# Transposes three steps behind their scores in a pipelined attention trunk on one core

## The chip, the core and the metric

The kernel runs on one core of one Trainium2 chip. The metric is device time in microseconds (us). Over three runs the kernel before took 768.53 us in the median (767.16 to 770.72).

The engines in what follows: PE is TensorE's matmul (PEld its weight load), DVE is VectorE, ACT ScalarE, POOL GpSimd, and SP is SyncE, which here only issues DMAs.

## What is computed

One layer of a hybrid decoder trunk: sequence 1024, model width 1024, all in float32. One input projection feeds three kinds of heads of width 64, their outputs are gated and mapped back, the input is added, and the sum is normalised.

```python
u = rms_norm(x, attn_norm)
dq, dk, dv, sq, ckv, iq, ik, iw, rq, rk, rv, gate = split(u @ w_in)
# A: six differential heads, causal
a = softmax(q0 @ k0.T) - lam * softmax(q1 @ k1.T)      # per head
o_a = rms_norm(a @ v) * (1 - lam_init)
# B: six sparse heads: an indexer scores keys, each query keeps its top 256 of them
score = sum_h(relu(iq_h @ ik.T) * iw_h);  sel = top_k(score, 256)
o_b = softmax(q_lat @ c_sel.T) @ c_sel @ w_uv
# C: four retention heads in chunks of 128
y = silu(gate) * concat(o_a, o_b, o_c)
out = rms_norm(x + y @ w_out, final_norm)
```

## The kernel before

Each float32 product is split into a high and a low half, so that one block of a gemm costs three matmuls (L130 to L132 for the input projection, L1003 to L1005 for the output projection). The program hands its streams of work to a scheduler that fixes every engine's order before the run, from program order and a simulation of when operands are ready. `interleave` shares the streams out by costs that are written in the table `K`. Its entry `bufs` is `NST, NP, NPQ, NW, NHL, NHALF, NY`, the numbers of buffers in seven pools; `NP` is that of `pp` (second softmaxes of the differential heads, every softmax of the sparse heads, L91's `ptile`) and `NPQ` that of `pq` (first softmaxes of the differential heads, and some tiles of the retention).

In time the stages follow each other so (`run`): the norm and load of the input to 51 us; first gemms and the indexer's scores to 160; then the six differential heads, the top-k search on DVE and ACT, and the other gemms side by side to about 500; the sparse heads for the second half of the queries beside the ties of the top-k, the output weights' loads and the start of the retention to 587; the sparse heads for the first half beside the rest of the retention and the first blocks of the output projection to 711; and the rest of the projection to the end.

Both kinds of attention go through `attend`, a software pipeline over steps. A step is one head and one block of 128 queries; two such blocks make a group (`GB`). At step t the program emits, in this order:

- the scores of step t into a PSUM tile `pS` (L718 in `diff`, L787 and L788 in `dsa`; two such tiles exist),
- the transposes of the probabilities of step t-2 into PSUM tiles `pB` (L678; two exist), each copied to the SBUF tile `pt` by ACT or DVE (L113, L115; `pt` has two buffers),
- `comb` of step t-1: reciprocals and scaling. For `diff` that is DVE's L743, POOL's scaling of `pq` (L744), and DVE's L745, L746 and L747, which forms the difference in `pp`; for `dsa` L801 and L803,
- `soft` of step t: a DVE instruction adds the mask and takes the row's extremum (L729, or L795 in `dsa`), ACT takes the exponential (L731, or L796),
- where step t-2 ended a group, the value product (L693) of that group: up to 15 matmuls from `pt` into a `pB` tile. In `dsa` DVE multiplies the result with the gate (L825).

The value product's matmuls keep their written order; everything else on PE is placed by the scheduler, with gemm matmuls between. `wide` (L298) borrows attention buffers early for raw weights. `project` loads the gated outputs as `yr` (L988, on SP's queue, where `out_weights` issues its loads of `w_out` at L969 and the heads issue their stacks at L383), splits them on ACT and multiplies (L1003).

Of the kernel before, what the change touches and what calls it, by code (L numbers as in the profile page):

```python
# [28 lines left out]
    0, 384, 768, 1152, 1536, 1664, 2176, 2248, 2504, 2760, 3016)  # L29
WA = 384 + 72  # L30
C_R = (C_RQ, C_RK, C_RV)
K = {'mk': 'up ky', 'mp': 's2 g5 g4', 'rt': ('hl', 'pq'), 's0': ('gg', 'ag', 'gg', 'ag', 'gg', 'ag', 'gg', 'ag'), 'xp': 2, 'bufs': (8, 3, 3, 5, 3, 4, 1), 'pp': (7,), 'rot': 0, 'order': 'g0 g1 k1 q1 k2', 'order2': 'q2 g2 rq g6 s0 ck g7 s1 M g3 rv rk | ', 'wd': 36, 'wt': 13, 'wg': 119, 'gw': 56, 'rw': 26, 'rx': 132, 'pw': 40, 'ow': 84, 'nf': 2, 'ev': 200, 'late': 8, 'de': ('aa', 'aa', 'aa'), 'da': 'ax', 'gd': (7, 4, 2), 'hlp': 'sqkk', 'tkp': '', 'vt': 'v', 'rs': 'x', 'nv': 1, 'dn': 'v', 'ws': 'gg', 'oe': ('av', 'gg'), 'one': 0, 'idx': (42, 40), 'iqs': 'iq2 iq3 q0 k0'}
NST, NP, NPQ, NW, NHL, NHALF, NY = K["bufs"]


# [33 lines left out]
class Trunk:  # L69
# [228 lines left out]
    def wide(self):  # L298
        self.dvw = []
        for k0 in range(0, KC, 2):  # L300
            tag, bufs = ("pq", NPQ) if k0 < 2 * NPQ else ("hl", NHL)
            raw = self.sb.tile([128, 2, WA], F, name=self.name("wr"), tag=tag, bufs=bufs)
            for j in ((0, 1), (1, 2)) if k0 < 2 else ((0, 2),):
                self.nc.scalar.dma_start(raw[:, j[0]:j[1]], self.i["w_dv"][
                    (k0 + j[0]) * 128:(k0 + j[1]) * 128].rearrange("(k p) c -> p k c", p=128))
            self.dvw.append(raw)

    def wsplit(self, c0, w):
        hs, ls = [], []
        if w == WA:  # L310
# [4 lines left out]
            ls = [big[2 + k // 2][:, k % 2] for k in range(KC)]  # L315
            self.split_w = lambda k: self.split(hs[k], ls[k], self.dvw[k // 2][:, k % 2], *K["s0"][k])
            return hs, ls
        n = 1024 // w
        for k0 in range(0, KC, n):
            h, l = (self.wtile("w" + x, [n, w]) for x in "hl")  # L320
            for j in range(0, n, n // 2):
                raw = self.rtile([n // 2, w])
                self.nc.sync.dma_start(raw, self.i["w_in"][0, (k0 + j) * 128:(k0 + j + n // 2) * 128,
                                                           c0:c0 + w].rearrange("(k p) c -> p k c", p=128))
                self.split(h[:, j:j + n // 2], l[:, j:j + n // 2], raw, *K["ws"])
            hs += [h[:, j] for j in range(n)]
# [3 lines left out]
    def evict(self, evac, *args):  # L330
        with self.tc.high_priority(offset=K["ev"]):
            evac(*args)
# [21 lines left out]
    def to_dram(self, key, n=2):  # L354
# [3 lines left out]
        def evac(half, ps):  # L358
            sl = slice(half * 512, half * 512 + 512)
            t = self.sb.tile([128, 2, 512], FR, name=self.name("hl"), tag="hl", bufs=NHL)  # L360
            if key[:2] in K["hlp"]:
                nc = self.nc
# [59 lines left out]
    def topk(self):  # L422
        nc = self.nc
        gd = K["gd"]
        ga = tuple(b for b in range(7, 1, -1) if b not in gd)
# [226 lines left out]
    def attend(self, pair, stages, GB=2, groups=(3, 2, 1, 0)):  # L652
        nc = self.nc
        steps = [(a, g, i) for a in range(2) for g in groups
                 for i in range(g * GB, g * GB + GB)]
        head, scores, soft, comb = stages
        pts, val = {}, {}
        W = GB * 128
        N = len(steps)
        hd = {}  # L660
        for t in range(N + 2):
            if t < N:
                a, g, i = steps[t]
                if a not in hd:
                    hd[a] = head(a)
                val[t] = scores(hd[a], i)
            if t >= 2:
                a, g, i = steps[t - 2]
                pr = val.pop(t - 2)
                if (g, a) not in pts:  # L670
                    pts[g, a] = self.sb.tile([128, NB, W], F, name=self.name("pt"), tag="pt", bufs=2)
                pt = pts[g, a]
                qo = (i - g * GB) * 128
                for k0 in range(0, i + 1, 4):
                    nk = min(4, i + 1 - k0)
                    p = self.pB((128, 4, 128))
                    for k in range(nk):
                        nc.tensor.transpose(p[:, k], pr[:, (k0 + k) * 128:(k0 + k + 1) * 128], self.ident)  # L678
                    self.cp(self.evac_eng[k0 // 4], pt[:, k0:k0 + nk, qo:qo + 128], p[:, :nk])
            if 0 <= t - 1 < N:  # L680
                val[t - 1] = comb(val[t - 1])
            if t < N:
                val[t] = soft(steps[t][2], val[t])
            if t >= 2 and steps[t - 2][2] % GB == GB - 1:
                a, g, i = steps[t - 2]
                o = self.pB((128, 128))
                h = 2 * pair + a
                vals = [self.v[:, k, h * 64:(h + 1) * 64] for k in range(i + 1)]
                with self.tc.manual_schedule(engines={mybir.EngineType.PE}):
                    for k in (i, *range(i)):  # L690
                        for u in (1, 0):
                            if k < i or u:
                                self.last = nc.tensor.matmul(  # L693
                                    o[u * 64:(u + 1) * 64], vals[k], pts[g, a][:, k, u * 128:(u + 1) * 128],
                                    start=k == (i if u else 0), stop=k == i - 1, skip_group_check=True)
                yield 0.5, (a, g, o)
            yield (steps[min(t, N - 1)][2] + 1) / 4.5, None
# [354 lines left out]
```

## Time and profile before

| | |
|---|---|
| median of three runs | 768.53 us (767.16 to 770.72) |
| profiled execution | 772.95 us, its span 771.2 us |
| PE busy | 718.2 us (93%) |
| PEld busy | 591.1 us (77%) |
| DVE busy | 559.9 us (73%) |
| ACT busy | 458.6 us (59%) |
| POOL busy | 310.4 us (40%) |
| chain that ended last | PE 62%, DVE 13%, DMA 8%, issue 7%, ACT 4%, POOL 4% |

Times of single instructions come from the one profiled execution. A busy share over the span is a mean over stages that differ; the page's 40 slices show DVE at nine tenths only from the eighth to the twenty-fourth, and PE near nine tenths through most of the span. "Waits" name the idle time in front of an instruction and the instruction that ended it.

### The profile page before, as it was taken

The numbers are of one execution on the slowest core, as the hardware profiler recorded it, in microseconds if no ns is written. First come the engines' busy times: TensorE is split into PE (matmuls) and PEld (weight loads), VectorE is DVE, ScalarE is ACT, GpSimd is POOL, SyncE is SP. The second block draws the span as 40 slices with busy tenths as digits, with TensorE's granted clock in tenths as the row PEclk, the third lists the DMA queues.
The fourth block names the chain that finished last, engine by engine and source line by source line (L and its number), as shares of the span: only waits on it lengthen the run. The fifth ranks groups of instructions, "written<-read, shape, count | busy, mean of one in ns | idle before, by whom it ended". The sixth has DMA issues, their size and how long they took to land.

```text
span 771.2 us, 12824 instructions
## 1 busy us (share of the span) xinstructions
PE 718.2 (93%) x4266; PEld 591.1 (77%) x4266; DVE 559.9 (73%) x1315; ACT 458.6 (59%) x1002; POOL 310.4 (40%) x343
## 2 busy tenths in 40 slices
PE   6999999999989999978889889999978999999996
PEld 5986788887878988756767668989756887777884
DVE  3684577989999989999889986426657775654443
ACT  4762555489687877786845655533355665653332
POOL 6422122434424539447347787337633332120000
PEclk9999999999999999999899989999979999999998
DMA  9716455472484344451383685565579964413441
GB/s 337 255 28 178 137 159 142 111 191 79 118 202 109 99 132 113 114 144 31 91 239 108 172 229 167 145 203 165 177 212 272 251 203 113 132 34 106 137 166 55
DMA packets 93618, 116.73 MB, mean 151 GB/s; under 512 B 11120, under 2 KB 62704, under 8 KB 93424
## 3 DMA queue, kind: packets, MB, share of 16 engines
q1 hardware_dynamic: 91152, 111.94, 50.8%
q10 hardware_dynamic: 2400, 3.97, 1.4%
q8 instruction: 34, 0.56, 0.3%
q14 instruction: 32, 0.26, 0.1%
HBM read 79.17 MB, written 36.18 MB: 150 GB/s over the span
## 4 chain that ended last, share of the span: by engine, by line
PE 62%; DVE 13%; DMA 8%; issue 7%; ACT 4%; POOL 4%; SPq 2%; ACTq 0%; DVEq 0%; POOLq 0%
PE pG L130 6%; PE pG L131 6%; PE pG L132 6%; PE pB L693 5%; PE pB L678 4%; PE pG L1003 4%; PE pG L1004 4%; PE pG L1005 4%; PE pS L272 3%; PE pG L347 2%; DVE jv L443 2%; PE pG L349 2%; PE pG L348 2%; PE pS L409 2%; PE pS L408 2%
## 5 line engine op out<-in xcount | busy, mean ns | idle before, releaser
L130 PE MATMUL pG<-uh,wh 128*128 128x512 f32 x352 | 142.5, 405 | 4.5 <-DVE gt L894 2.1
L132 PE MATMUL pG<-uh,wl 128*128 128x512 f32 x352 | 141.2, 401 | 1.7 <-POOL wl L123 1.7
L131 PE MATMUL pG<-ul,wh 128*128 128x512 f32 x352 | 140.4, 399 | 1.3 <-DVE ul L255 1.3
L123 POOL TENSOR_TENSOR wl<-wr,wh 128x512 fp32r<-128x512 f32 x56 | 79.9, 1443 | 84.4 <-PE pG L131 73.8
L457 ACT ACTIVATE ja<-sc,tk_c 128x896 int8<-128x896 f32 (+2 forms) x93 | 83.3, 896 | 22.3 <-DVE tk_c L464 16.5
L113 ACT ACTIVATE pt<-pB 128x512 f32<-128x512 f32 (+2 forms) x120 | 58.9, 496 | 41.9 <-PE pB L678 41.7
L130 PEld LDWEIGHTS pG<-uh,wh 128*128 128x128 f32 x352 | 67.5, 192 | 19.3 <-DVE gt L894 2.4
L132 PEld LDWEIGHTS pG<-uh,wl 128*128 128x128 f32 x352 | 67.4, 192 | 16.7 <-POOL wl L123 2.5
L131 PEld LDWEIGHTS pG<-ul,wh 128*128 128x128 f32 x352 | 67.4, 191 | 15.5 <-DVE ul L255 3.3
L678 PE MATMUL pB<-ident,pp 128*128 128x128 f32 x432 | 73.4, 288 | 4.6 <-DVE gt L825 1.9
L693 PE MATMUL pB<-pt,v 128*64 128x128 f32 x864 | 68.0, 294 | 7.4 <-ACT pt L113 6.8
L693 PEld LDWEIGHTS pB<-pt,v 128*64 128x64 f32 x864 | 55.3, 143 | 18.9 <-ACT pt L113 9.5
L443 DVE TENSOR_SCALAR_CACHE_REDUCE jv<-sc,tk_c 128x640 bf16<-128x640 f32 (+4 forms) x81 | 69.1, 853 | 0.9
L119 POOL TENSOR_SCALAR wh<-wr 128x512 fp32r<-128x512 f32 x56 | 40.3, 723 | 69.9 <-DMA wr<-in_w_in_dram 50.8
L678 PEld LDWEIGHTS pB<-ident,pp 128*128 128x128 f32 x432 | 51.7, 145 | 20.4 <-issue 8.5
L744 POOL TENSOR_SCALAR pq<-pq,mx 128x896 f32<-128x896 f32 (+7 forms) x48 | 39.2, 816 | 58.5 <-DVE mx L743 46.1
L347 PE MATMUL pG<-wh,uh 128*128 128x256 f32 x192 | 55.4, 290 | 0.7 <-POOL wh L119 0.7
L411 ACT ACTIVATE pp<-pS 128x1024 f32<-128x1024 f32 (+5 forms) x48 | 36.5, 760 | 31.5 <-PE pS L409 31.5
L348 PE MATMUL pG<-wl,uh 128*128 128x256 f32 x192 | 55.0, 287 | 0.0
L349 PE MATMUL pG<-wh,ul 128*128 128x256 f32 x192 | 54.4, 284 | 0.0
L747 DVE SCALAR_TENSOR_TENSOR pp<-pp,mx,pq 128x896 f32<-128x896 f32 (+7 forms) x48 | 51.1, 1065 | 4.4 <-POOL pq L744 3.6
L416 DVE SCALAR_TENSOR_TENSOR sc<-pp,iw,sc 128x1024 f32<-128x1024 f32 (+5 forms) x42 | 43.5, 1048 | 14.6 <-ACT pp L411 14.2
(234 smaller groups left out, 1731.4 us busy)
## 6 DMA issues: line engine op xcount, KB each, us to landing
wr<-in_w_in_dram SPq DMA_DIRECT2D x56, 256.0 KB, 3.1
st<-qdq SPq DMA_DIRECT2D x24, 256.0 KB, 4.2
st<-qkk SPq DMA_DIRECT2D x18, 256.0 KB, 6.1
qiq<-hl SPq DMA_DIRECT2D x16, 256.0 KB, 3.5
st<-qiq SPq DMA_DIRECT2D x8, 512.0 KB, 3.4
wr<-in_w_out_dram SPq DMA_DIRECT2D x16, 256.0 KB, 3.3
xr<-in_x_dram SPq DMA_DIRECT2D x8, 512.0 KB, 3.6
yr<-yd SPq DMA_DIRECT2D x7, 512.0 KB, 4.1
```

The source lines that it names most:

```text
L113: self.nc.scalar.activation(out, in_, AF.Copy)
L123: (self.nc.vector if e2 == "v" else self.nc.gpsimd).tensor_tensor(lo, src, hi.bitcast(F), OP.subtract)
L130: mm(ps, wh, xh, start=start, stop=False)
L131: mm(ps, wh, xl, start=False, stop=False)
L132: mm(ps, wl, xh, start=False, stop=stop)
L347: mm(ps, uh, hs[k], start=k == 0, stop=False)
L348: mm(ps, uh, ls[k], start=False, stop=False)
L349: mm(ps, ul, hs[k], start=False, stop=k == KC - 1)
L443: nc.vector.tensor_scalar(jv[:, :nv[b]], hb if b == 7 and bit >= 16 else sc[b], t, 0.0, op0=op, op1=OP.add, accum_out=cnt[:, j:j + 1])
L457: nc.scalar.activation(ja[:, :nv[b]], sc[b], AF.Sign, bias=cut(b), scale=-1.0, accum_out=cnt[:, cols[b]:cols[b] + 1])
L678: nc.tensor.transpose(p[:, k], pr[:, (k0 + k) * 128:(k0 + k + 1) * 128], self.ident)
L693: self.last = nc.tensor.matmul(o[u * 64:(u + 1) * 64], vals[k], pts[g, a][:, k, u * 128:(u + 1) * 128], start=k == (i if u else 0), stop=k ...
```

## The change

In `attend` a constant `L = 3` sets the distance of the transposes behind the scores, where 2 was written. A finished group is remembered in `done`, handed to `ready` at the next step, and its value product is emitted there: one step after the group's last transposes, at the same place in the step. The loop runs two more steps to empty the pipeline. `bufs` gives `pp` four buffers where it had three, and `pq` two where it had three. `wide` takes the third pair of raw weights from the `pp` pool instead of from `pq`. In the changed file L678 is L681, L693 is L698, and lines from 700 on stand five lower.

```diff
@@ -29,7 +29,7 @@
     0, 384, 768, 1152, 1536, 1664, 2176, 2248, 2504, 2760, 3016)
 WA = 384 + 72
 C_R = (C_RQ, C_RK, C_RV)
-K = {..., 'bufs': (8, 3, 3, 5, 3, 4, 1), ...}
+K = {..., 'bufs': (8, 4, 2, 5, 3, 4, 1), ...}
 NST, NP, NPQ, NW, NHL, NHALF, NY = K["bufs"]
 
 
@@ -298,7 +298,7 @@
     def wide(self):
         self.dvw = []
         for k0 in range(0, KC, 2):
-            tag, bufs = ("pq", NPQ) if k0 < 2 * NPQ else ("hl", NHL)
+            tag, bufs = (("pq", NPQ), ("pq", NPQ), ("p", NP), ("hl", NHL))[k0 // 2]
             raw = self.sb.tile([128, 2, WA], F, name=self.name("wr"), tag=tag, bufs=bufs)
             for j in ((0, 1), (1, 2)) if k0 < 2 else ((0, 2),):
                 self.nc.scalar.dma_start(raw[:, j[0]:j[1]], self.i["w_dv"][
@@ -658,15 +658,18 @@
         W = GB * 128
         N = len(steps)
         hd = {}
-        for t in range(N + 2):
+        L = 3
+        done = None
+        for t in range(N + L + 1):
             if t < N:
                 a, g, i = steps[t]
                 if a not in hd:
                     hd[a] = head(a)
                 val[t] = scores(hd[a], i)
-            if t >= 2:
-                a, g, i = steps[t - 2]
-                pr = val.pop(t - 2)
+            ready, done = done, None
+            if L <= t < N + L:
+                a, g, i = steps[t - L]
+                pr = val.pop(t - L)
                 if (g, a) not in pts:
                     pts[g, a] = self.sb.tile([128, NB, W], F, name=self.name("pt"), tag="pt", bufs=2)
                 pt = pts[g, a]
@@ -677,12 +680,14 @@
                     for k in range(nk):
                         nc.tensor.transpose(p[:, k], pr[:, (k0 + k) * 128:(k0 + k + 1) * 128], self.ident)
                     self.cp(self.evac_eng[k0 // 4], pt[:, k0:k0 + nk, qo:qo + 128], p[:, :nk])
+                if i % GB == GB - 1:
+                    done = (a, g, i)
             if 0 <= t - 1 < N:
                 val[t - 1] = comb(val[t - 1])
             if t < N:
                 val[t] = soft(steps[t][2], val[t])
-            if t >= 2 and steps[t - 2][2] % GB == GB - 1:
-                a, g, i = steps[t - 2]
+            if ready:
+                a, g, i = ready
                 o = self.pB((128, 128))
                 h = 2 * pair + a
                 vals = [self.v[:, k, h * 64:(h + 1) * 64] for k in range(i + 1)]
```

**PE, first head of the third pair of differential heads, the group of its last two query blocks.** The group's value product `L693` (`L698`) stands among scores (`L718`, `L723`), transposes (`L678`, `L681`) and gemm matmuls (`L130` to `L132`). Before:

```order
L678 MATMUL pB_3346<-ident,pp_3215 128x128 x4
L678 MATMUL pB_3352<-ident,pp_3215 128x128 x4
L718 MATMUL pS_3463<-st_3128,st_3125 128x384
L132 MATMUL pG_3573<-uh,wl_3488 128x512
L130 MATMUL pG_3573<-uh,wh_3487 128x512
L131 MATMUL pG_3573<-ul,wh_3487 128x512
L132 MATMUL pG_3573<-uh,wl_3488 128x512
L718 MATMUL pS_3510<-st_3121,st_3118 128x512
L693 MATMUL pB_3370<-pt_3298,v_158 64x128 x15
L678 MATMUL pB_3466<-ident,pp_3319 128x128 x4
```

After:

```order
L723 MATMUL pS_3560<-st_3106,st_3103 128x128
L131 MATMUL pG_3544<-ul,wh_3426 128x512
L132 MATMUL pG_3544<-uh,wl_3427 128x512
L130 MATMUL pG_3544<-uh,wh_3426 128x512
L131 MATMUL pG_3544<-ul,wh_3426 128x512
L132 MATMUL pG_3544<-uh,wl_3427 128x512
L723 MATMUL pS_3562<-st_3113,st_3110 128x128
L698 MATMUL pB_3509<-pt_3354,v_158 64x128 x15
L681 MATMUL pB_3564<-ident,pp_3375 128x128 x4
```

Before, the transposes of the group's last step (`pB_3346`, `pB_3352`, both from `pp_3215`) stand six rows ahead of the fifteen value matmuls. After, the last transposes that fill `pt_3354` (into `pB_3453`) stand 58 rows ahead of them.

**PE, the first matmul of the output projection**, where the sparse heads' first half of steps ends. `S` tiles of `L787` (`L792`) are scores, `woh` and `wol` the split output weights. Before:

```order
L787 MATMUL pS_6516<-st_6442,st_6440 128x512
L788 MATMUL pS_6516<-st_6444,st_6440 128x512
L787 MATMUL pS_6516<-st_6442,st_6440 128x256
L788 MATMUL pS_6516<-st_6444,st_6440 128x256
L693 MATMUL pB_6271<-pt_6258,v_5586 64x128 x3
L678 MATMUL pB_6496<-ident,pp_6453 128x128 x4
L787 MATMUL pS_6580<-st_6575,st_6573 128x512
L1003 MATMUL pG_6224<-woh,yh_6221 128x512
L1004 MATMUL pG_6224<-wol,yh_6221 128x512
```

After:

```order
L792 MATMUL pS_6158<-st_6137,st_6138 128x512
L793 MATMUL pS_6158<-st_6137,st_6138 128x512
L681 MATMUL pB_6146<-ident,pp_6102 128x128 x4
L1008 MATMUL pG_6195<-woh,yh_6192 128x512
L1009 MATMUL pG_6195<-wol,yh_6192 128x512
L506 MATMUL pG_6271<-rt_5614,bd 128x256
L792 MATMUL pS_6199<-st_6137,st_6138 128x128
L793 MATMUL pS_6199<-st_6137,st_6138 128x128
```

Before, the first projection matmul (`pG_6224`) stands behind the first score of the sixth step of the stage for the first half of the queries. After, it (`pG_6195`) stands before the last two scores of the stage ahead of that, seven score tiles earlier.

**SP's queue around the load of `yr`** (`L988`, `L993`), which that matmul needs. Before:

```order
L969 DMA wr_6044<-in_w_out_dram 128x512
L383 DMA st_6575<-qkk_4189 128x1024
L383 DMA st_6577<-qkk_4189 64x1024
L830 DMA yd_67<-gt_6146 128x1x128
L969 DMA wr_6068<-in_w_out_dram 128x512
L830 DMA yd_67<-gt_6146 128x1x128
L980 DMA fn_6215<-in_final_norm_dram 128x1024
L988 DMA yr_6217<-yd_68 128x3x128
L969 DMA wr_6072<-in_w_out_dram 128x512
```

After:

```order
L974 DMA wr_5939<-in_w_out_dram 128x512
L974 DMA wr_5994<-in_w_out_dram 128x512
L828 DMA gt_6182<-gd_3969 64x2x128
L835 DMA yd_67<-gt_5967 128x1x128 x2
L985 DMA fn_6186<-in_final_norm_dram 128x1024
L993 DMA yr_6188<-yd_68 128x3x128
L998 DMA xr_6190<-in_x_dram 128x1024
L974 DMA wr_5998<-in_w_out_dram 128x512
```

The load of `yr` stands behind 13 of the 16 loads of `w_out` before and behind 11 of them after, and `L383`'s loads of the last stage's first stacks stand ahead of it before, behind it after.

## Rows read from the trace of the kernel before

**Rows 1.** The page, busy time of each engine over the span, with instructions.
```profile
PE 718.2 (93%) x4266; PEld 591.1 (77%) x4266; DVE 559.9 (73%) x1315; ACT 458.6 (59%) x1002; POOL 310.4 (40%) x343
```

**Rows 2.** Busy time by stretch: PE, PEld, DVE, ACT, POOL, granted clock, DMA share.
```profile
190.00:320.00 130.00, 125.67 (x792) 105.78 (x791) 122.67 (x334) 101.17 (x236) 64.46 (x79) 0.99 0.48 126
320.00:454.00 134.00, 114.73 (x615) 89.34 (x614) 125.96 (x300) 91.36 (x212) 82.66 (x78) 0.92 0.51 137
454.00:515.00 61.00, 60.11 (x435) 52.57 (x431) 27.38 (x69) 31.02 (x75) 29.29 (x32) 1.00 0.60 177
560.00:590.00 30.00, 23.60 (x129) 16.67 (x129) 17.93 (x61) 17.58 (x46) 8.26 (x8) 0.77 0.84 234
590.00:711.00 121.00, 118.44 (x907) 96.22 (x907) 77.65 (x173) 68.87 (x150) 30.90 (x42) 1.00 0.52 150
```

**Rows 3.** PE's waits, 190 to 454 us: total us, times, longest.
```profile
PE pB L693 <- ACT pt L113: 6.3, 2, 3.5
PE pS L718 <- DVE mx L729: 4.3, 7, 0.9
...
PE pS L718 <- DMA qsq<-hl: 2.5, 1, 2.5
```

**Rows 4.** DVE's waits, 190 to 454 us.
```profile
DVE pp L729 <- PE pS L718: 2.6, 1, 2.6
...
DVE pq L729 <- PE pS L718: 2.3, 3, 1.7
...
DVE pp L747 <- POOL pq L744: 0.6, 1, 0.6
```

**Rows 5.** DVE's timeline, 363 to 382 us: start, length, instruction, idle before.
```profile
374.16 0.29 DVE L729 CUSTOM_DVE_ANT_0 pq<-pS,cb 128x128 f32<-128x128 f32 x1 [1.74 <-PE pS L718]
...
379.91 0.69 DVE L729 CUSTOM_DVE_ANT_0 pp<-pS,cb 128x512 f32<-128x512 f32 x1 [0.93 <-PE pB L678]
```

**Rows 6.** PE's timeline, 364 to 370 us.
```profile
369.01 1.39 PE L693 MATMUL pB<-pt,v 128*64 128x128 f32 x10 [3.51 <-ACT pt L113]
```

**Rows 7.** The page's costliest groups: two of POOL's.
```profile
L123 POOL TENSOR_TENSOR wl<-wr,wh 128x512 fp32r<-128x512 f32 x56 | 79.9, 1443 | 84.4 <-PE pG L131 73.8
...
L744 POOL TENSOR_SCALAR pq<-pq,mx 128x896 f32<-128x896 f32 (+7 forms) x48 | 39.2, 816 | 58.5 <-DVE mx L743 46.1
```

**Rows 8.** DVE's waits, 515 to 711 us.
```profile
DVE pp L795 <- PE pB L678: 8.0, 14, 1.6
```

**Rows 9.** PE's waits, 454 to 590 us.
```profile
PE pS L787 <- DVE mx L795: 1.9, 5, 0.7
PE pG L1003 <- ACT yh L113: 1.7, 1, 1.7
...
PE pB L693 <- ACT pt L113: 0.5, 1, 0.5
```

**Rows 10.** PE's waits, 590 to 720 us.
```profile
PE pS L787 <- DVE mx L795: 1.1, 2, 0.8
PE pB L678 <- ACT pt L115: 0.7, 1, 0.7
PE pB L693 <- DVE pt L115: 0.6, 1, 0.6
```

**Rows 11.** SyncE's DMA issues, 571 to 583 us.
```profile
573.87 0.33 SPq L969 DMA_DIRECT2D wr<-in_w_out_dram  x1
...
582.28 0.46 SPq L988 DMA_DIRECT2D yr<-yd  x1
```

**Rows 12.** PE's timeline, 571 to 592 us.
```profile
571.79 0.41 PE L788 MATMUL pS<-st,st 128*128 128x512 f32 x1
...
589.32 0.50 PE L1003 MATMUL pG<-woh,yh 128*128 128x512 f32 x1 [1.68 <-ACT yh L113]
```

**Rows 13.** ACT's timeline, 586 to 590 us.
```profile
588.74 0.52 ACT L113 ACTIVATE yh<-yr 128x384 fp32r<-128x384 f32 x1 [2.23 <-DMA yr<-yd]
```

More of the change, by code (lines that the diff above doesn't have):

```diff
@@ L31 @@
 C_R = (C_RQ, C_RK, C_RV)
-K = {'mk': 'up ky', 'mp': 's2 g5 g4', 'rt': ('hl', 'pq'), 's0': ('gg', 'ag', 'gg', 'ag', 'gg', 'ag', 'gg', 'ag'), 'xp': 2, 'bufs': (8, 3, 3, 5, 3, 4, 1), 'pp': (7,), 'rot': 0, 'order': 'g0 g1 k1 q1 k2', 'order2': 'q2 g2 rq g6 s0 ck g7 s1 M g3 rv rk | ', 'wd': 36, 'wt': 13, 'wg': 119, 'gw': 56, 'rw': 26, 'rx': 132, 'pw': 40, 'ow': 84, 'nf': 2, 'ev': 200, 'late': 8, 'de': ('aa', 'aa', 'aa'), 'da': 'ax', 'gd': (7, 4, 2), 'hlp': 'sqkk', 'tkp': '', 'vt': 'v', 'rs': 'x', 'nv': 1, 'dn': 'v', 'ws': 'gg', 'oe': ('av', 'gg'), 'one': 0, 'idx': (42, 40), 'iqs': 'iq2 iq3 q0 k0'}
+K = {'mk': 'up ky', 'mp': 's2 g5 g4', 'rt': ('hl', 'pq'), 's0': ('gg', 'ag', 'gg', 'ag', 'gg', 'ag', 'gg', 'ag'), 'xp': 2, 'bufs': (8, 4, 2, 5, 3, 4, 1), 'pp': (7,), 'rot': 0, 'order': 'g0 g1 k1 q1 k2', 'order2': 'q2 g2 rq g6 s0 ck g7 s1 M g3 rv rk | ', 'wd': 36, 'wt': 13, 'wg': 119, 'gw': 56, 'rw': 26, 'rx': 132, 'pw': 40, 'ow': 84, 'nf': 2, 'ev': 200, 'late': 8, 'de': ('aa', 'aa', 'aa'), 'da': 'ax', 'gd': (7, 4, 2), 'hlp': 'sqkk', 'tkp': '', 'vt': 'v', 'rs': 'x', 'nv': 1, 'dn': 'v', 'ws': 'gg', 'oe': ('av', 'gg'), 'one': 0, 'idx': (42, 40), 'iqs': 'iq2 iq3 q0 k0'}
 NST, NP, NPQ, NW, NHL, NHALF, NY = K["bufs"]
```

## The prediction

> **What bounds the kernel now.** I read the busy times first, then the stretches, then the waits of each stretch's bound. Over the span PE is busy 93% [rows 1], which would make it the bound everywhere. By stretch it isn't [rows 2]. From 190 to 454 us DVE is busy 122.67 of 130 and 125.96 of 134 us, 248.6 of 264, so that it idles 15.4; PE idles 4.3 + 19.3 = 23.6 there. From 454 to 515 PE is full (60.11 of 61) and DVE under half. From 560 to 590 nothing is full: PE 23.60 of 30, DVE 17.93, at a granted clock of 0.77, under the upper of PE's two levels (2.4 GHz is 1.00); there a chain of dependent steps sets the pace. From 590 to 711 PE is full again (118.44 of 121). So a saved wait counts on DVE in the stage of the differential heads, on PE behind it, and on whichever engine the chain stands at between 560 and 590.
>
> On PE's number the Trainium skill (Perfetto Trace Analysis, Identifying the Most-Contended Engine) says that the matmul row's busy share is a poor measure of how close an engine is to its limit, and that the weight loads' share is better. In the stretch that is full by its matmuls weight loads are busy 96.22 of 121, 80%, so 80% is about what "full" reads as here; by the rule as it stands 23% of the span (771.2 - 591.1 = 180 us) would be open, by the row 771.2 - 591.1/0.80 = 32 us. Neither enters the sum.
>
> **The change part by part.** All of it is counted against the profiled execution of 772.95 us; the median of the runs is 768.53, so its sums are multiplied by 0.9943 at the end.
>
> *The value product one step later, 190 to 454 us.* PE waited 6.3 us, twice, for ACT's copy into `pt` [rows 3]; one of the two is a 3.51 us wait at 369.01 [rows 6]. With the product a step behind its transposes the copy has a step more: in the order the last transposes stand 58 rows ahead of the product where they stood six ahead. I expect both waits gone. But DVE is the bound, so only what DVE lost through them counts: 1.74 us at 374.16 (it waits for a score that PE issued late) and 0.93 at 379.91 (for a transpose that frees a `pp` buffer) [rows 5]. Value -2.7; ends 0 (DVE has other work queued and the idle only moves) and -6.3 (PE's whole wait).
>
> *What stays there.* PE's waits for score tiles, 4.3 us in seven [rows 3], come from two `pS` tiles, which the change leaves at two: 0. DVE's longest wait, 2.6, is for a score that PE had to hold 2.5 for a DMA [rows 3, 4]; the loads of the stacks aren't altered, but any of them could shift: 0, ends -2.6 and +2.6.
>
> *The transposes three steps behind, with four `pp`.* A `pp` tile lives from `soft` of step t to the transposes of the same step. In program order two live at a time with distance 2, three with distance 3. Three buffers for two, or four for three, leave one spare either way. So DVE's waits for a `pp` buffer don't get rarer by the count alone; a transposed step merely finds `comb` done for longer, and in 190 to 454 PE's rows show no wait of a transpose for `comb` at all. Value 0; its cost, that PE's work at the end of the third pair comes two steps later, falls in 454 to 515, where PE is full of gemm matmuls that can go first: 0, end +5 if they run out (about two steps' transposes and products at the mean PE idle of such a step, by the 6.3 of [rows 3] the size of thing that can stand open).
>
> *Two `pq` for three.* Only one `pq` is alive in program order when the next is taken, so two suffice if POOL scales in time: POOL's scaling takes 816 ns in the mean, behind weight splits of 1443 [rows 7]. DVE waited 0.6 once for it [rows 4]. In DVE's order the median number of rows between the reciprocal that starts POOL and the combine falls from 15 to 10, and combines at seven rows or fewer go from 6 of 48 to 12. Ten rows at DVE's mean of 559.9/1315 = 0.43 us [rows 1] are 4.3 us, more than 1443 + 816 ns = 2.26. So the cover holds in most: the 0.6 doubles with the tight ones, +0.6. Ends: 0, and twelve tight combines that each lose 2.26 less three rows of cover (1.3), 12 x 0.96 = +11.5.
>
> *`wide` with a `pp` buffer.* The order on PE is the same up to about 190 us, so the early gemms hide it: 0. Should the `pp` tile come free late, the first of the sparse indexer's work would be held by one raw load; by the 2.5 us that a load held PE [rows 3], +2.5.
>
> *Sparse heads, 515 to 590.* PE waits 1.9 us in five for DVE to release a score tile, and 0.5 for ACT's copy into `pt` [rows 9]. DVE is late there because its own first instruction waits for transposes, 8.0 us in 14 [rows 8]: the transposes sit on PE behind the scores. With distance 3 they are of older, finished steps, and the order has them four score tiles behind their scores in the median, three before. So I take both waits as gone, -2.4; ends 0 (one spare buffer as before) and -6.4 (all of PE's 30 - 23.60 idle [rows 2]).
>
> *Sparse heads, 590 to 711.* Three waits of the same kinds, 1.1 + 0.7 + 0.6 [rows 10]: -2.4; ends 0 and -2.6 (PE's whole idle there).
>
> *The first projection matmul, which the order brings forward.* Before, it stood behind the first score of the next stage's sixth step and still waited 1.7 us [rows 9, 12] for ACT's split of `yr`, and ACT for the DMA until 588.74 [rows 13]. Its load was issued at 582.28 [rows 11], so it took 6.5 us to land. After, the load stands behind 11 `w_out` loads instead of 13, which is behind the issue at 573.87 [rows 11] and the stores and the `fn` load that keep their place there, about 575.5. It lands at 575.5 + 6.5 = 582.0, and the matmul could start 0.6 later (589.32 - 588.74), at 582.5. The matmul now stands seven score tiles earlier on PE, about where the score at 571.79 ends [rows 12], 572.2. PE is in order: scores of the two last steps and all their softmaxes queue behind it. If nothing else moves, it stalls 582.5 - 572.2 = 10.3 us. Against this: PE itself gets there later, since it waits at earlier places for the same DMAs and softmaxes (DMA engines are busy 0.84 [rows 2]), and part of the stall takes the place of the 6.4 us that PE idles there anyway. Ends -1.7 (the load is in time) and +10.3; I take +1.7, the old wait again, as the nearest row of the same instruction.
>
> *The sum.* -2.7 + 0.6 - 2.4 - 2.4 + 1.7 = -5.2: 772.95 - 5.2 = 767.75, times 0.9943 = 763.4 us, told as 763.
>
> **The rivals.**
>
> *Nothing happens.* DVE paces the stage from 190 to 454 and PE only waits somewhere else; the counts of spare buffers are the same as before, and the waits of 0.5 to 1.9 us reappear one instruction further on. Then 768.5, give or take 2. For it: DVE's 15.4 us of idle in 264, of which the value product explains 2.7. Against it: those 2.7 and the 4.8 behind 515 stand on the engine that bounds. The Trainium skill (Perfetto Trace Analysis, Optimization Strategy) says that a gap which repeats on the engine that should be full can mean that too few buffers are there for the next tile. By that rule the gap to mend is the one that repeats, PE's seven waits for `pS` (4.3 us), which the change doesn't touch; of the added `pp` buffer DVE's rows show one wait of 0.93 in the stage. The rule speaks for this rival.
>
> *The change doesn't do what it says* belongs to it: for the differential heads the scheduler put the transposes a median of four score tiles behind their scores in both orders, so that the distance written there is not the one executed.
>
> *The slow chain fills up.* If the older transposes free the pipeline between 560 and 590, PE's 6.4 us go, and its clock rises from 0.77 to 1.00, 23.60 x 0.23 = 5.4 more. With -2.7 and -2.4: -16.9, 756.05 x 0.9943 = 752. For it: four engines under 80% there. Against it: DMA at 0.84, which the change doesn't relieve.
>
> *Slower: the early projection matmul blocks PE.* The place is the matmul on `woh`, `yh` before the last two scores of the first sparse stage; the price is the 10.3 us above with no wait of 515 to 590 saved: -2.7 + 0.6 - 2.4 + 10.3 = +5.8, 778.75 x 0.9943 = 774.3. It decides once the stall exceeds about 8 us. For it: the order moves the matmul by seven score tiles, but its load by two of `w_out`. Against it: the load's 6.5 us came in a stretch with DMAs at 0.84 and can shrink.
>
> *Slower: `pq` runs short.* The +11.5 above in place of +0.6: 778.65 x 0.9943 = 774.2. It decides if POOL is behind a split at most of the tight combines. Against it: 0.6 us in all before.
>
> **How the numbers follow.** Forecast 0.36, nothing 0.24, the chain fills 0.15, the projection blocks 0.16, `pq` short 0.09. About 0.5% is what a measurement of this kernel can tell from no change: 764.7 and 772.4. The forecast's own range is 758 to 768, 0.26 of its 0.36 below 764.7. Faster 0.26 + 0.15 = 0.41; same 0.10 + 0.24 = 0.34; slower 0.16 + 0.09 = 0.25. The range goes from 752, the filled chain, to 777, 3 us above the slower rivals for their loose prices.
>
> **What the profile after would show.** Right: no wait of the value product (L698) for ACT's copy over 1 us between 190 and 454, and DVE's idle there near 12.7 instead of 15.4; fewer than 14 waits of L800 for transposes; L1008 waiting under 4 us. Wrong: L1008 waiting 8 or more; L752 waiting for POOL several times; the dsa stages' lengths unchanged with their waits merely renamed; or a stack's load that lands later and holds PE in the differential stage, which I cost at nothing.

## The result, and the profile after

The changed kernel took 777.51 us in the median of four runs (776.02 to 782.97) against 769.41 (767.16 to 770.72) in the same comparison: a ratio of 1.0108, 95% interval 1.0068 to 1.0148. It is slower by about 1%, where 763 was forecast. Its profiled execution took 776.35 us, against 772.95 before. So the two traces show 3.4 us of a difference that is 8.1 in the medians; what they show is where some of it went, and the ratios of the experiments carry the rest.

The page, busy time of each engine over the span, answering to [rows 1]:

```profile
PE 718.0 (93%) x4266; PEld 591.8 (76%) x4266; DVE 561.8 (73%) x1315; ACT 455.0 (59%) x1002; POOL 308.6 (40%) x343
```

Busy time by stretch, columns as in [rows 2]: PE, PEld, DVE, ACT, POOL, granted clock, DMA share, GB/s.

```profile
190.00:320.00 130.00, 122.39 (x763) 102.08 (x762) 121.11 (x337) 100.07 (x238) 62.60 (x79) 0.96 0.46 125
320.00:454.00 134.00, 121.09 (x660) 94.71 (x660) 128.77 (x298) 91.75 (x212) 85.49 (x80) 0.95 0.53 143
454.00:515.00 61.00, 60.02 (x435) 52.48 (x430) 27.14 (x72) 31.20 (x76) 27.39 (x30) 1.00 0.52 148
560.00:590.00 30.00, 25.06 (x155) 18.91 (x154) 21.56 (x68) 16.40 (x45) 10.54 (x13) 0.88 0.92 260
590.00:711.00 121.00, 114.62 (x859) 92.76 (x859) 74.72 (x174) 66.00 (x148) 25.42 (x36) 0.99 0.48 139
```

PE's busy time times its granted clock is, roughly, the work done at full clock (good to about a microsecond a row: the clock is a mean over the stretch, idle time included). From 190 to 320 us it was 125.67 x 0.99 = 124.4 before and is 122.39 x 0.96 = 117.5; from 320 to 454 it was 105.6 and is 115.0. Together PE did 2.5 us more by 454. From 590 to 711 it was 118.4 and is 113.5. The stretch in between, of before and then of after:

```profile
515.00:560.00 45.00, 43.09 (x345) 37.40 (x344) 29.33 (x88) 17.87 (x48) 29.20 (x41) 1.00 0.60 183
```

```profile
515.00:560.00 45.00, 39.24 (x312) 34.93 (x310) 28.89 (x79) 17.05 (x45) 30.69 (x42) 0.93 0.67 208
```

Here 43.1 us of work became 36.5; in the next stretch 18.2 became 22.1 [rows 2]. From 515 to 711 PE lost 6.6 - 3.9 + 4.9 = 7.6 us, three times what it had gained. Two single waits stand in these stretches, and the granted clock is at or near the lower level behind each: 0.50 from 555.7 to 560 us, 0.58 from 610.9 to 615.

```profile
555.70 2.15 PE L681 MATMUL pB<-ident,pp 128*128 128x128 f32 x8 [4.90 <-DVE gt L830]
610.89 0.75 PE L596 MATMUL pG<-rt 64*128 64x128 f32 x8 [3.76 <-ACT rt L589]
```

PE's waits from 190 to 454 us (total, times, longest), answering to [rows 3]:

```profile
PE pS L723 <- DVE mx L734: 5.5, 5, 2.3
PE pS L723 <- DVE jv L443: 3.3, 2, 3.0
...
PE pB L698 <- ACT pt L113: 0.2, 1, 0.2
```

The value product's 6.3 us are 0.2. The waits for score tiles stayed. DVE's waits in the same stretch, answering to [rows 4]:

```profile
DVE tk_n L462 <- ACT ja L457: 5.0, 4, 2.7
DVE pq L734 <- PE pS L723: 2.5, 3, 1.3
...
DVE pp L734 <- PE pB L681: 0.3, 1, 0.3
```

DVE's idle went from 15.4 to 264 - 121.11 - 128.77 = 14.1. PE's waits from 515 to 590, and from 590 to 711, answering to [rows 9] and [rows 10]:

```profile
PE pB L681 <- DVE gt L830: 7.5, 3, 4.9
...
PE pB L698 <- ACT pt L113: 0.8, 2, 0.5
...
PE pG L1008 <- ACT yh L113: 0.5, 1, 0.5
```

```profile
PE pG L596 <- ACT rt L589: 3.8, 1, 3.8
PE pS L792 <- DVE mx L800: 1.1, 1, 1.1
```

The wait of 7.5 us was 1.9 before. It is a transpose that wants a `pB` tile which still holds a value product; DVE multiplies that with a gate, and waited 4.1 us in all for gates to be loaded. The load is issued with the product, so a step later than before, but that isn't shown to be the reason: with the sparse heads' old loop the same wait is 3.9 us in e1, 4.4 in k2 and 6.0 in j1 (runs below). The 3.8 us are for a tile of the retention. DVE's waits for transposes in the sparse stages, 8.0 us in 14 before [rows 8], became 12.7 in 13; from 590 to 711 they are:

```profile
DVE pp L800 <- PE pB L681: 10.6, 10, 2.8
```

DVE's timeline at the end of the differential heads (the last combine, then the first sparse softmax):

```profile
498.88 0.48 DVE L752 SCALAR_TENSOR_TENSOR pp<-pp,mx,pq 128x256 f32<-128x256 f32 x1
511.33 0.56 DVE L800 CUSTOM_DVE_ANT_0 pp<-pS,sc 128x384 f32<-128x384 f32 x1 [11.97 <-PE pS L793]
```

The first sparse softmax waited 12 us for its score. Against the kernel before that is no loss. There DVE idled 16.3 us between the same two instructions, and the first sparse softmax came 4.3 us later:

```profile
497.44 0.48 DVE L747 SCALAR_TENSOR_TENSOR pp<-pp,mx,pq 128x256 f32<-128x256 f32 x1
509.38 0.69 DVE L507 TENSOR_SCALAR f<-pB 128x512 f32<-128x512 f32 x1 [11.45 <-PE pB L506]
511.44 0.75 DVE L513 SCALAR_TENSOR_TENSOR f<-f,c_diff_norm,f 128x512 f32<-128x512 f32 x1 [1.36 <-ACT f L509]
515.67 0.56 DVE L795 CUSTOM_DVE_ANT_0 pp<-pS,sc 128x384 f32<-128x384 f32 x1 [3.48 <-PE pS L788]
```

In PE's order 191 matmuls of the retention's gemms are left behind the first sparse score, where 288 were left before. But that count hangs on one matmul: before, the first of a score's two matmuls was issued alone, 15 us ahead of the second, and behind the second 191 are left too.

```profile
500.38 0.34 PE L787 MATMUL pS<-st,st 128*128 128x384 f32 x1
515.29 0.34 PE L788 MATMUL pS<-st,st 128*128 128x384 f32 x1
```

### The profile page after: what moved, and what is told of

It reads as the page before. It is cut to its first block, busy times and chain, and to the rows that moved or that the text cites. A ratio compares the mean times of both kernels' runs of the same rounds, so it can differ in the third digit from the quotient of the medians.

```text
span 774.6 us, 12837 instructions
## 1 busy us (share of the span) xinstructions
PE 718.0 (93%) x4266; PEld 591.8 (76%) x4266; DVE 561.8 (73%) x1315; ACT 455.0 (59%) x1002; POOL 308.6 (40%) x343
## 4 chain that ended last, share of the span: by engine, by line
PE 53%; DVE 23%; DMA 10%; issue 6%; ACT 3%; POOL 2%; SPq 1%; DVEq 0%; ACTq 0%; POOLq 0%
DVE jv L443 5%; PE pG L130 4%; PE pG L132 4%; PE pG L131 4%; PE pB L698 4%; PE pG L1008 4%; PE pG L1009 4%; PE pG L1010 4%; DVE pp L752 3%; PE pB L681 3%; PE pS L272 3%; DMA st<-qkk 2%; PE pG L348 2%; PE pG L347 2%; DVE pp L734 2%
## 5 line engine op out<-in xcount | busy, mean ns | idle before, releaser
L130 PE MATMUL pG<-uh,wh 128*128 128x512 f32 x352 | 143.9, 409 | 5.5 <-DVE gt L899 3.7
L132 PE MATMUL pG<-uh,wl 128*128 128x512 f32 x352 | 141.1, 401 | 2.9 <-POOL wl L123 2.9
L130 PEld LDWEIGHTS pG<-uh,wh 128*128 128x128 f32 x352 | 68.1, 194 | 21.4 <-issue 4.0
L681 PE MATMUL pB<-ident,pp 128*128 128x128 f32 x432 | 72.5, 286 | 9.7 <-DVE gt L830 7.5
L132 PEld LDWEIGHTS pG<-uh,wl 128*128 128x128 f32 x352 | 67.8, 193 | 17.6 <-POOL wl L123 3.3
L681 PEld LDWEIGHTS pB<-ident,pp 128*128 128x128 f32 x432 | 53.5, 146 | 23.1 <-DVE gt L830 8.2
L698 PE MATMUL pB<-pt,v 128*64 128x128 f32 x864 | 64.9, 284 | 2.5 <-ACT pt L113 1.8
L698 PEld LDWEIGHTS pB<-pt,v 128*64 128x64 f32 x864 | 52.3, 138 | 14.4 <-issue 6.1
L347 PE MATMUL pG<-wh,uh 128*128 128x256 f32 x192 | 55.1, 288 | 0.8 <-DVE mx L748 0.6
L411 ACT ACTIVATE pp<-pS 128x1024 f32<-128x1024 f32 (+5 forms) x48 | 36.5, 761 | 31.4 <-PE pS L409 31.4
L723 PE MATMUL pS<-st,st 128*128 128x512 f32 (+3 forms) x144 | 45.1, 383 | 10.5 <-DVE mx L734 5.5
L349 PE MATMUL pG<-wh,ul 128*128 128x256 f32 x192 | 54.4, 284 | 0.0
```

The lines of the kernel that those rows point to most:

```text
L130: mm(ps, wh, xh, start=start, stop=False)
L132: mm(ps, wl, xh, start=False, stop=stop)
L347: mm(ps, uh, hs[k], start=k == 0, stop=False)
L349: mm(ps, ul, hs[k], start=False, stop=k == KC - 1)
L698: self.last = nc.tensor.matmul(o[u * 64:(u + 1) * 64], vals[k], pts[g, a][:, k, u * 128:(u + 1) * 128], start=k == (i if u else 0), stop=k ...
```

## The experiments

All kernels but the one before and k3 have the new buffers unless told otherwise. "First sparse" is the start of the first sparse softmax in the trace, "left" the number of retention gemm matmuls (L347 to L349) that stand on PE behind the first matmul of a sparse score, and "left, third" behind the third such matmul.

| kernel | weight | loops, buffers | ratio to before, 95% | first sparse, us | left | left, third |
|---|---|---|---|---|---|---|
| before | 36 | old, pp 3, pq 3 | 1 | 515.7 | 288 | 191 |
| changed | 36 | new in both | 1.0108 (1.0068 to 1.0148) | 511.3 | 191 | 191 |
| e1 | 36 | new in differential heads | 1.0053 (1.0025 to 1.0081) | 513.9 | 191 | 191 |
| e2 | 36 | new in sparse heads | 0.9916 (0.9887 to 0.9946) | 486.5 | 360 | 191 |
| e3 | 36 | old | 0.9906 (0.9876 to 0.9937) | 488.4 | 360 | 191 |
| e4 | 36 | distance 3, no delay | 1.0127 (1.0097 to 1.0158) | 518.8 | 240 | 191 |
| f1 | 36 | old, pp 3, pq 2 | 1.0128 (1.0093 to 1.0162) | 516.4 | 191 | 191 |
| f2 | 36 | distance 2, delay, differential | 1.0102 (1.0069 to 1.0134) | 518.3 | 191 | 191 |
| g1 | 36 | new in third pair | 0.9990 (0.9959 to 1.0020) | 481.3 | 384 | 365 |
| g2 | 36 | new in first two pairs | 1.0006 (0.9974 to 1.0038) | 515.9 | 191 | 191 |
| j1 | 32 | old | 1.0158 (1.0134 to 1.0181) | 531.7 | 24 | 0 |
| j2 | 32 | new in both | 1.0268 (1.0223 to 1.0314) | 535.9 | 0 | 0 |
| j3 | 40 | old | 0.9924 (0.9896 to 0.9953) | 474.5 | 384 | 384 |
| j4 | 40 | new in both | 0.9923 (0.9899 to 0.9946) | 481.3 | 384 | 384 |
| k1 | 36 | new in both, drains free | 1.0100 (1.0064 to 1.0136) | 517.1 | 191 | 191 |
| k2 | 34.5 | old | 1.0014 (0.9994 to 1.0035) | 505.1 | 191 | 191 |
| k3 | 40 | old, pp 3, pq 3 | 1.0040 (1.0024 to 1.0057) | 492.4 | 360 | 240 |
| k4 | 36 | as f2, drain free | 1.0013 (0.9986 to 1.0039) | 511.5 | 191 | 191 |
| m2 | 36 | new in both, retention later | 1.0224 (1.0193 to 1.0256) | 489.5 | 348 | 348 |
| n1 | 32 | new in both, retention later | 1.0167 (1.0139 to 1.0196) | 505.5 | 254 | 254 |

**Which part loses.** After the traces, theory A was that the sparse heads' loop loses; B, the buffers; C, any new order. The edit of e1 (e2 has the two pairs of numbers exchanged, e3 has (2, 0) for both, e4 has (3, 0)):

```diff
-        L = 3
+        L, V = (3, 1) if len(groups) == 4 else (2, 0)
-        for t in range(N + L + 1):
+        for t in range(N + L + V):
                     done = (a, g, i)
+                    if not V:
+                        ready, done = done, None
```

e1: 

> New distance (three steps, value product one later) in the differential heads alone; the sparse heads keep two steps and no delay; buffers as in the changed kernel. Theory A (the sparse stages lose: in the profile after PE idles 6.2 us more than before from 515 us on, and 3.1 us less from 190 to 454): about 766, 3 us under before. Theory B (the buffers, two first softmaxes and four second ones, cost the time): as the changed kernel, 775 to 778. Theory C (every edit gives the scheduler another order, and that alone moves the time by up to 1% either way): anywhere from 763 to 777, without a pattern over the four kernels.

e2: 

> New distance in the sparse heads alone; the differential heads keep two steps; buffers as in the changed kernel. Theory A: the loss of the sparse stages without the gain of the differential heads, 776 to 780. Theory B: 775 to 778 as well. Theory C: anywhere from 763 to 777.

e3: 

> Both kinds of heads as before, only the buffers (four pp, two pq, and the raw weights' third pair in pp). Theory A: 769, within 3 us of before. Theory B: 775 to 778, all of the loss. Theory C: 763 to 777.

e4: 

> Transposes three steps behind in both, the value product in the step of its last transposes as before; buffers as in the changed kernel. If the loss sits in the delayed value product of the sparse heads (its gate load is issued later and its PSUM buffer held longer: PE waited 4.9 us for that in the profile after): 769 or less. If it sits in the distance of three: 776 to 778. Theory C: 763 to 777.

Theory A fell, though the traces' losses stand in the sparse stages: the new loop in the sparse heads alone costs nothing (0.9916 against 0.9906), in the differential heads alone it costs 1.5% of e3. B fell as well: the buffers alone gain 0.94%. And the distance without the delay, e4, isn't better. Before against changed mixes two opposite effects. Against e3, which differs from the changed kernel in the loops alone, PE's work is about 4 us behind by 454 us (117.5 + 115.0 against 126.1 + 110.9) and about 7 from 515 to 711; the two spans differ by 10.6 us (774.6 and 764.0). e1 is behind in the same way. So an edit in the differential heads loses in their own stage and in the stages behind it.

In e3's trace the differential heads end, and the sparse heads begin, earlier than in either kernel (DVE's last combine and first sparse softmax):

```profile
483.22 0.49 DVE L754 SCALAR_TENSOR_TENSOR pp<-pp,mx,pq 128x256 f32<-128x256 f32 x1
488.44 0.56 DVE L802 CUSTOM_DVE_ANT_0 pp<-pS,sc 128x384 f32<-128x384 f32 x1 [4.73 <-PE pB L681]
```

That is 23 us earlier than in the changed kernel.

**Buffer, delay, or the tail of the last pair.** Theory D: the fourth `pp` gains as a spare, and distance three uses it up. Theory E: the longer drain of the third pair makes the sparse heads start late. f1 is e3 with `pp` 3; f2 is e3 with (2, 1) in the differential heads; g1 and g2:

```diff
-        L = 3
+        L, V = (3, 1) if len(groups) == 4 and pair == 2 else (2, 0)    # g1; g2: pair < 2
```

f1: 

> Loops as before (distance two, no delay), pq two, but pp three instead of four: one spare pp buffer as in the kernels of before and of the change, where the kernel with only the new buffers has two. Theory D (the fourth pp gained its 0.94% by being spare, and distance three in the differential heads uses it up): 1.000 to 1.010 of before, 770 to 778. Theory E (the loss of the new distance sits in the tail of the differential heads: their last steps come late and the sparse heads start late; the spare buffer has no part in that): this says nothing of the gain's source; if the gain came from two pq or from other order, 0.99, about 765.

f2: 

> New buffers, distance two, only the value product of the differential heads a step later. Theory D: still two spare pp, so the gain stays: 0.990 of before, 765. Theory E: the tail is one step longer, half of what distance three and the delay add: about 0.998, 770.

g1: 

> New buffers; distance three and the delay only in the third pair of differential heads, everything else as before. Its order on PE is that of the kernel with only the new buffers up to the start of the third pair. Theory E: nearly all of the loss, 1.003 to 1.008 of before, with the last differential combine near 499 us instead of 483. Theory D: a third of it, about 0.996.

g2: 

> New buffers; distance three and the delay only in the first two pairs. Its order on PE is that of the changed kernel up to the start of the third pair. Theory E: nothing or little of the loss, 0.990 to 0.994 of before. Theory D: two thirds of it, about 1.000, with PE's work at 320 us behind that of the kernel with only the new buffers by the 8 us that the changed kernel is behind there.

f1 against e3: with two `pq`, the fourth `pp` is worth 2.2%, and f1 at 1.0128 lies a little above D's range. f1 against before: with three `pp`, the third `pq` is worth 1.3%, together with `wide`'s raw weights, which f1 takes from `pp`. f2 keeps two spare `pp` and still loses 2.0% of e3, so D can't be the whole cause. E fell by its own sign: in g1 the last differential combine stands at 477.3, not near 499, the sparse heads begin at 481.3, earlier than in e3, and the time is 0.8% longer all the same. The loss isn't one pair's: g1 and g2 lose 0.8 and 1.0% of e3. Part of f2's is seen, in PE's waits from 165 to 480 us:

```profile
PE pS L725 <- DMA st<-qdk: 10.2, 3, 6.1
PE pS L725 <- DMA st<-qdq: 4.0, 1, 4.0
```

These 14.2 us are for stacks that the differential heads load; in the changed kernel PE's waits of that kind from 190 to 454 are 0.5 us, and 3.0 that its profile puts down to DVE and e1's, at the same place, to such a load. f2's delay of a product doesn't touch that load; that the new order put SP's issues elsewhere is likely, and no run here isolates it.

**Order alone.** Against theory C stands F: distance and delay cost 1 to 2% whatever the order. j1 to j4 change nothing but a weight, in e3's loops and in the changed ones:

```diff
-'wd': 36
+'wd': 32    # j1 (old loops), j2 (new); j3, j4: 40
```

j1: 

> New buffers, loops as before (the kernel that ran at 0.9906 of before), with the weight of the differential heads' stream in the interleaving at 32 in place of 36: nothing but the scheduler's order moves, from the 1111th row of PE on. Theory F (distance and delay cost 1 to 2% whatever the order around them): within 0.5% of 0.991. Theory C (the scheduler's order moves the time by about 1% with any edit, and 0.9906 was a lucky order): anywhere from 0.990 to 1.013, more likely near 1.003, the mean of what the nine kernels have shown.

j2: 

> The changed kernel (1.0108 of before) with the same weight, 32 for 36; its order on PE moves from row 1099 on. Theory F: 1.006 to 1.016. Theory C: anywhere from 0.990 to 1.013, and as likely below the kernel with the old loops at that weight as above it.

j3: 

> New buffers, loops as before, weight 40 for 36; its order on PE moves from row 1449 on. Theory F: within 0.5% of 0.991. Theory C: 0.990 to 1.013.

j4: 

> The changed kernel with weight 40 for 36; a larger weight also makes up for the cost that its three longer drains add to that stream (2 steps of 0.44 in each of three pairs). Theory F: 1.006 to 1.016. Theory C: 0.990 to 1.013. If the loss comes from that added cost in the interleaving: 0.995 or less.

F fell. At weight 40 the new loops cost nothing (0.9923 against 0.9924), at 36 2.0%, at 32 1.1%: distance and delay have no fixed price. The same number moves the old loops by 2.5%. C's direction held and its size didn't: j1 and j2 lie above its 1.013. j4's busy times in three stretches:

```profile
190.00:320.00 130.00, 120.98 (x781) 101.23 (x779) 122.83 (x337) 101.08 (x240) 64.57 (x79) 1.00 0.48 128
320.00:454.00 134.00, 116.60 (x633) 89.93 (x634) 128.66 (x310) 94.04 (x217) 84.89 (x79) 0.94 0.52 141
515.00:590.00 75.00, 71.61 (x573) 61.59 (x571) 49.01 (x146) 36.26 (x95) 38.84 (x51) 1.00 0.72 215
```

Its differential stage is no better than the changed kernel's (PE 121.0 and 109.6 us of work at full clock against 117.5 and 115.0). But from 515 to 590 PE works 71.6 us at a clock of 1.00; the changed kernel's row stands under m2 below. Its sparse heads start early (DVE's last combine and first sparse softmax):

```profile
480.50 0.85 DVE L752 SCALAR_TENSOR_TENSOR pp<-pp,mx,pq 128x256 f32<-128x256 f32 x1
481.27 0.55 DVE L800 CUSTOM_DVE_ANT_0 pp<-pS,sc 128x384 f32<-128x384 f32 x1
```

An early start isn't enough, though: g1's first sparse softmax starts at the same 481.3, and its PE works 66.43 us at 0.91 from 515 to 590.

**Is it the charge?** Each pair's loop runs two steps longer at its end, each charged 0.44 in the interleaving, 4% of a pair's charge (20.9 to 21.8). Theory G: so the differential heads fall behind.

```diff
-            yield (steps[min(t, N - 1)][2] + 1) / 4.5, None
+            yield (steps[min(t, N - 1)][2] + 1) / 4.5 if t < N + 2 else 0.0, None
```

k1: 

> The changed kernel at weight 36; the steps that the new loop adds at the end of each pair cost nothing in the interleaving (the charge of a pair is that of the old loop). Theory G (the added charge puts the differential heads behind): 0.990 to 0.996 of before, the last differential combine before 490 us. Theory F (distance and delay cost by themselves): 1.006 to 1.016 as the changed kernel. Theory C (order alone): anywhere from 0.990 to 1.027.

k2 is e3 at weight 34.5. 

> New buffers, loops as before, weight 34.5 in place of 36: the share that the changed loops' higher charge leaves (a pair's charge of 20.9 becomes 21.8, and 36 x 20.9/21.8 = 34.5). Theory G: half or more of the loss, 1.000 to 1.011, the last differential combine past 490 us. Theory F: 0.990 to 0.994. Theory C: 0.990 to 1.016.

k3 is the kernel before at weight 40. 

> The kernel before, buffers and loops untouched, weight 40 for 36. Theory G: its differential heads end at 497 us behind gemms that end at 484, so a larger share gains: 0.990 to 0.996. If the fourth pp buffer is what allows the gain: 0.998 to 1.005. Theory C: 0.990 to 1.016.

k4 is f2 with the same edit as k1. 

> New buffers, distance two, only the value product of the differential heads a step later (1.0102 of before), now with the added drain step free of charge. Theory G: 0.990 to 0.998. Theory F: 1.006 to 1.014. Theory C: 0.990 to 1.016. Its order on PE is the same as that of the charged one up to row 1430.

G fell for the change itself: k1 stays at 1.0100. It may hold in part elsewhere: k2 loses 1.1% of e3 by the share alone, and k4 gets back 0.9 of f2's 2.0%. k3 shows that a weight of 40 is no gain by itself: it costs the kernel before 0.4%, and the old loops with the new buffers run the same at 40 as at 36.

**Is it the cover of the sparse heads' first stage?** Over the table to k4, time goes with "left" and "first sparse": 360 or 384 left and a start before 490 us in all five at or under 0.999, 191 or fewer in nine of the eleven above 1.0006 (e4 and k3 are the others). "Left" is a loose guide, since in before, e2, e3, e4 and k3 it counts from an early score that stands alone; counted from the third matmul, e2 and e3 have the same 191 as most of the kernels that lose. Theory H: the retention's gemms cover that stage's waits, and orders that spend them earlier pay there. m2 (n1 at weight 32) moves two of them:

```diff
-... s1 M g3 rv rk | '
+... s1 M g3 | rv rk'
```

m2: 

> The changed kernel at weight 36 with the gemms of the retention's keys and values moved from the differential heads' stream of gemms to the stream beside the sparse heads; PE's order is unchanged up to its row 1831, and 348 retention gemm matmuls stand behind the first sparse score in place of 191. Theory H (cover for the sparse heads' first stage): 0.990 to 0.998 of before, the first sparse softmax before 495 us instead of 511. Theory F (distance and delay cost by themselves): 1.006 to 1.016. Theory C (order without a pattern): 0.990 to 1.027.

n1: 

> The same move in the changed kernel at weight 32 (1.0268 of before): 254 matmuls left in place of 0, PE's order unchanged up to row 1812. Theory H: near the kernel before, which has 288: 0.998 to 1.010. Theory F: 1.020 to 1.030. Theory C: 0.990 to 1.027.

m2 contradicts H as the account of the whole time, and bears it out for the stage. Busy times from 515 to 590 and 590 to 650, of the changed kernel and of m2, whose orders on PE are the same up to about 480 us, and then of e3 (with its differential stage):

```profile
515.00:590.00 75.00, 64.31 (x464) 53.83 (x463) 50.45 (x144) 33.45 (x89) 41.24 (x55) 0.91 0.77 229
590.00:650.00 60.00, 55.84 (x440) 45.33 (x439) 39.20 (x92) 33.38 (x75) 16.04 (x23) 0.97 0.69 194
```

```profile
515.00:590.00 75.00, 71.20 (x597) 61.58 (x597) 52.83 (x149) 39.95 (x97) 35.30 (x45) 1.00 0.61 181
590.00:650.00 60.00, 47.23 (x290) 36.11 (x287) 30.53 (x59) 24.26 (x51) 18.75 (x25) 0.80 0.59 180
```

```profile
190.00:320.00 130.00, 126.08 (x803) 105.58 (x802) 125.96 (x359) 106.18 (x251) 65.57 (x81) 1.00 0.52 136
320.00:454.00 134.00, 116.71 (x642) 90.10 (x640) 124.55 (x287) 90.45 (x208) 86.95 (x80) 0.95 0.51 139
515.00:590.00 75.00, 66.72 (x482) 54.00 (x480) 47.89 (x143) 36.19 (x92) 35.50 (x49) 0.93 0.76 207
590.00:650.00 60.00, 57.43 (x473) 46.01 (x473) 41.15 (x90) 35.41 (x77) 18.96 (x24) 1.00 0.67 179
```

From 515 to 590 PE's work at full clock goes from 64.31 x 0.91 = 58.5 to 71.2 us: 12.7 us more are done there with the later gemms. From 590 to 650 it goes from 54.2 to 37.8, 16.4 back, with PE idle for 12.8 of 60 us; of PE's waits from 600 to 720 in m2, 7.2 us are for tiles of the retention, whose chain started with its gemms, and 3.5 for the copy of one value product. n1 got back 1.0% of j2 and stays at 1.0167 where H said 0.998 to 1.010. So the gemms kept for that stage are shown to set how much PE does in it; that they decide the total isn't.

No kernel of these beats e3 clearly. e2, e3, j3 and j4 lie within 0.2% of each other, all with the new buffers, and two of them with the old loops throughout.

## Why the prediction was wrong, step by step

*The value product:* the mechanism came. PE's two waits went, 6.3 to 0.2, and DVE's idle fell by 1.3 where 2.7 was the term. PE was 2.5 us further by 454, about the size told, but that is luck: e3, whose old loops keep these waits (6.6 us in three), is 7 us further than the kernel before (237.0 against 230.0). The gain of the stage came with the buffers, and the loops took more than half of it back.

```profile
PE pB L700 <- ACT pt L113: 6.6, 3, 2.9
```

*The step that failed* is the price of the new loops: -2.7 for the product, -2.4 and -2.4 for the sparse stages, +1.7 for the projection, and for the longer pipeline "Value 0; its cost, that PE's work at the end of the third pair comes two steps later, falls in 454 to 515, where PE is full of gemm matmuls that can go first: 0". Together that is -5.8. Measured against e3, which has the same buffers and the old loops, the new loops cost 2.0% at this weight, about +15 us: 1.5% in the differential heads alone (e1), 0.1% in the sparse heads alone (e2). PE did stay full to 515 (60.02 of 61), as told; the loss stands before and behind that stretch, about 4 us by 454 and 7 from 515 to 711. All terms were waits of one order, taken out with the rest of the order left as it was. The scheduler gave the edit another order, with other waits in it, and that was put at nothing; at a weight of 40 the same loops cost nothing. It isn't the third pair's end either: g2, whose third pair has the old loop, loses 1.0% of e3.

*The sparse stages,* two terms of -2.4: the new loop there is worth nothing (e2 against e3). Of the small waits that I counted, those for a score tile from 515 to 590 went (1.9 us); the others stayed about as they were, and larger ones came: 7.5 us where 1.9 had been for gates, 3.8 for the retention. Of the signs of being right, "fewer than 14 waits of L800 for transposes" came true by number, 13, while their time rose from 8.0 to 12.7 us.

*The buffers* were costed at +0.6 (two `pq`) and 0 (four `pp` as one spare either way). All of them together measure -0.94% under the old loops (e3), about -7 us. Against before, f1 measures +1.28% for two `pq` with three `pp` (and `wide`'s edit), 9.9 us of 771, within the end of +11.5 that I gave to a rival; but DVE waited for POOL's scaling twice in its trace from 165 to 480, 1.7 us in all, so this is no proof of that rival's mechanism. e3 against f1 measures -2.2% for the fourth `pp` where the old loops leave it spare. Both are sums over another order each, not prices of a buffer.

*The first projection matmul:* it waited 0.5 us, not 10.3; the rival built on it didn't come. The sum had a slip here too: the old wait of 1.7 us coming again is no change against before, 0 and not +1.7, and what was measured is -1.2.

*The rivals:* the time fell on the slower side, but neither slower rival is what happened. The rival that was missing: the scheduler gives any edit another order, and an order moves this kernel by up to 2.5% (j1 and e3) with nothing but a weight changed. The range of 752 to 777 had been built from waits of one order, and the measured 777.5 lies outside it.

*What stays open:* why the scheduler's order for the new loops is a bad one at weight 36 and not at 40. Its sparse heads start 23 us later than e3's, but still 4 us earlier than those of the kernel before, which is faster; and in g1, which starts early, 0.8% is lost without a place that these runs name. The added charge isn't the reason (k1).

## What to carry to other kernels

Where a scheduler sets the order, compare an edit at two or three settings of an unrelated weight before believing its price: here one edit cost 1.1, 2.0 and 0.0% at three weights. Gemms moved from one stage to the next raised PE's work in the one by 12.7 us and cost 16.4 behind it (m2), so read such a move over all stages; and don't judge it by a count behind one matmul, which may stand alone. And a trace of before against after adds up every part of a change: here the buffers gained and the loops lost. Undoing the parts one at a time, and reading each trace against the run that differs in that part alone, told them apart.

## What the runs showed that was not expected

A wait on PE can cost more than it lasts. In the changed kernel PE waited 2.99 us in front of a score (start, length, instruction, idle before):

```profile
213.03 0.39 PE L130 MATMUL pG<-uh,wh 128*128 128x512 f32 x1
216.41 1.08 PE L723 MATMUL pS<-st,st 128*128 128x512 f32 x2 [2.99 <-DVE jv L443]
217.29 0.63 PE L131 MATMUL pG<-ul,wh 128*128 128x512 f32 x1
217.72 0.63 PE L132 MATMUL pG<-uh,wl 128*128 128x512 f32 x1
...
222.38 0.40 PE L131 MATMUL pG<-ul,wh 128*128 128x512 f32 x1
```

and the granted clock of the time behind it, and of the time behind that, is:

```profile
217.30:222.00 4.70, 4.70 (x13) 3.64 (x13) 4.37 (x12) 2.34 (x4) 0.00 (x0) 0.50 0.90 212
222.40:225.80 3.40, 3.40 (x25) 2.59 (x24) 0.43 (x4) 2.17 (x6) 2.19 (x3) 1.00 0.57 166
```

For 4.7 us PE ran at 1.2 GHz: its 128x512 matmuls start 0.43 us apart where they start 0.23 apart at the upper level (below), so eleven of them took 2.2 us more. The wait and what followed it cost over 5 us. In e3 the same stage has a wait of 1.26 us, and the matmuls behind it kept their pace:

```profile
221.48 0.64 PE L725 MATMUL pS<-st,st 128*128 128x512 f32 x2 [1.26 <-DMA st<-qdk]
221.96 0.39 PE L131 MATMUL pG<-ul,wh 128*128 128x512 f32 x1
222.19 0.39 PE L132 MATMUL pG<-uh,wl 128*128 128x512 f32 x1
```

The waits of 4.90 and 3.76 us above have the lower clock behind them as well, and so has e1's wait of 3.19 us at the same place (0.50 from 217.5 to 222). The prediction used the clock only in the rival of the filled chain; in its sum every wait counted at its length. The 2.99 us are probably the sign that it named last, a stack's load that lands later: e1's profile names that load in front of its 3.19 us, and the changed kernel's a DVE instruction that the score doesn't read.
